# Walking the tiles of a DMA-filled kernel from the last rows to the first

## The chip, the cores and the metric

The kernel runs on one core of one Trainium2 chip. The time is that of one execution on the device, in microseconds; medians of several executions are quoted with their number. The record marks each run fast or slow by its clock and its distance from the fastest run. Data go by DMA: 16 engines move packets between the chip's main memory (HBM), which holds x and the output, and the on-chip memory (SBUF). A packet is one contiguous piece; here each transfer has one for each of the 128 partitions of SBUF.

## The reference

```python
B, S, D = 8, 512, 2048                    # x: (8, 512, 2048) float32, gamma: (2048,)
x_rep = np.repeat(x, 2, axis=1)           # each row twice: (8, 1024, 2048)
rms = np.sqrt((x_rep ** 2).mean(axis=-1, keepdims=True) + 1e-6)
return (x_rep / rms * gamma[None, None, :]).astype(np.float32)
```

It is an RMS norm of 4096 rows of 8 KB whose result is written twice, so 33.55 MB come in and 67.11 MB go out.

## The kernel before

Eight tiles of 512 rows go through three row buffers. A partition holds four neighbouring rows, so a tile is one contiguous block of 4 MB in x and of 8 MB in the output. All large transfers are issued by SyncE (`nc.sync`), in program order.

```python
K = 4                                             # P = 128 partitions, R = 2
# ...
x_t = x.rearrange("b s d -> (b s) d").rearrange("(n p k) d -> n p k d", p=P, k=K)
out_t = out.rearrange("b s d -> (b s) d").rearrange("(n p j) d -> n p (j d)", p=P, j=K * R)
# ...
rows = ctx.enter_context(tc.tile_pool(name="rows", bufs=3))
# ...
def load(i, eng, parts=1):
    y = rows.tile([P, K * R, D], f32, name="y")
    step = K // parts
    for k in range(0, K, step):
        at = K * (R - 1) + k
        eng.dma_start(out=y[:, at : at + step, :], in_=x_t[i, :, k : k + step, :])
    ys.append(y)

def store(i, k0, k1):
    nc.sync.dma_start(
        out=out_t[i, :, R * k0 * D : R * k1 * D],
        in_=ys[i][:, R * k0 : R * k1, :].rearrange("p j d -> p (j d)"),
    )
# ... (square, scale, repeat) ...
def compute(i):
    for k in range(K):
        scale(i, k, square(i, k))                 # ScalarE squares, VectorE scales
    repeat(i, 0, K // 2, nc.scalar.copy)          # second copy of each row
    repeat(i, K // 2, K, nc.vector.tensor_copy)
# ...
load(0, nc.sync, parts=2)
# ... (gamma) ...
load(1, nc.sync)
load(2, nc.sync)
# ...
loads_after = {2: (3, 4, 5), 4: (6, 7)}
for i in range(ntiles):
    compute(i)
    store(i, 0, K)
    for j in loads_after.get(i, ()):
        load(j, nc.sync)
```

The text counts loads and stores from one, in the order of issue: load 3 is `load(2)`. On the DMA queue they stand as loads 1 to 3, stores 1 to 3, loads 4 to 6, stores 4 and 5, loads 7 and 8, stores 6 to 8. The five places where the kind changes are called seams.

## Time and profile before

| | before |
|---|---|
| time, median of 3 | 239.42 us (239.32 to 239.43) |
| span of the profiled execution | 237.9 us |
| VectorE busy, ScalarE busy | 96.5 us, 101.0 us |
| share of the DMA queue of x and the output | 98.5% |
| data moved over the span | 423 GB/s |
| packets of 16, 32, 64 KB, median | 611, 1213, 2418 ns |

The table says that the 16 DMA engines are full and that no compute engine is busy for half the time. The prediction shows the lines for this. The last row comes from the packet records of the trace, which give size, start and duration of each packet. One more view: the issues of SyncE in the timeline of before (start, time from the first issue's start to the last one's end, engine and line, what, how many).

```profile
0.72 8.20 SPq L52 DMA_DIRECT2D y<-in_x_dram  x4
...
27.05 24.67 SPq L56 DMA_DIRECT2D out_dram<-y  x3
...
52.84 39.05 SPq L52 DMA_DIRECT2D y<-in_x_dram  x3
...
115.86 12.72 SPq L56 DMA_DIRECT2D out_dram<-y  x2
...
140.24 19.73 SPq L52 DMA_DIRECT2D y<-in_x_dram  x2
...
160.08 36.66 SPq L56 DMA_DIRECT2D out_dram<-y  x3
```

These six groups are the six stretches between the five seams. An issue is not the start of the transfer: the second group of loads is issued from 52.84 us on, but its first packet starts at 90.4 us, behind the stores.

### The profile page before, as it was taken

To read this page: it belongs to the slowest core of one execution; us is meant where nothing else is said; L and a number is where in the kernel's file an instruction comes from. 1 tells how busy PE (TensorE), PEld (TensorE's weight loads), DVE (VectorE), ACT (ScalarE), POOL (GpSimd) and SP (SyncE) were. 2 spreads that over 40 slices of the span, in tenths; PEclk is the share of its full clock that TensorE was granted. 3 is DMA by queue.
4 is the path that set the end of the run, shared out by engine and by line. 5 is a ranking of instruction groups with operands and counts; after the bars stand their busy time and mean duration, and the time that the engine had idled before them with its cause. 6 is when DMAs were issued, how large, how long until landed. Compare 5 with 4: busy or idle time off the path is not lost.

```text
span 237.9 us, 287 instructions
## 1 busy us (share of the span) xinstructions
DVE 96.5 (41%) x73; ACT 101.0 (42%) x106; POOL 2.5 (1%) x5
## 2 busy tenths in 40 slices
DVE  0049999960000000059999960000199990000000
ACT  2697999900000000099999920000599960000000
POOL 0030000000000000000000000000000000000000
DMA  7999998989899998999998999989998989999994
GB/s 265 436 446 441 441 441 353 530 353 496 386 452 430 397 485 353 441 441 441 441 518 364 464 419 430 452 369 430 435 518 364 518 364 485 397 452 430 408 474 176
DMA packets 2464, 100.69 MB, mean 423 GB/s; under 512 B 279, under 2 KB 285, under 8 KB 286
## 3 DMA queue, kind: packets, MB, share of 16 engines
q1 hardware_dynamic: 2448, 100.66, 98.5%
q14 instruction: 2, 0.02, 0.0%
q10 hardware_dynamic: 14, 0.01, 0.0%
HBM read 33.56 MB, written 67.11 MB: 423 GB/s over the span
## 4 chain that ended last, share of the span: by engine, by line
DMA 58%; ACT 12%; DVE 9%; issue 1%; POOLq 1%; ACTq 1%; SPq 0%
DMA y<-in_x_dram 33%; DMA out_dram<-y 21%; ACT sq L64 8%; DVE y L74 7%; DMA gamma_b<-in_gamma_dram 4%; ACT y L81 3%; DVE y L81 2%; ACT rms L68 1%; POOLq L136 1%; ACTq L95 1%; DVE rstd L73 0%; POOLq L96 0%; SPq L56 0%
## 5 line engine op out<-in xcount | busy, mean ns | idle before, releaser
L64 ACT ACTIVATE sq<-y 128x2048 f32<-128x2048 f32 x32 | 59.7, 1865 | 87.8 <-DMA y<-in_x_dram 87.8
L74 DVE SCALAR_TENSOR_TENSOR y<-y,rstd,gamma_b 128x2048 f32<-128x2048 f32 x32 | 75.3, 2352 | 4.1 <-POOL gamma_b L96 3.0
L73 DVE RECIPROCAL rstd<-rms 128x1 f32<-128x1 f32 x32 | 5.0, 158 | 94.6 <-ACT rms L68 94.3
L81 ACT COPY y<-y 128x4096 f32<-128x4096 f32 x8 | 28.7, 3590 | 1.4 <-DVE y L74 1.4
L81 DVE COPY y<-y 128x4096 f32<-128x4096 f32 x8 | 18.3, 2294 | 0.3
L68 ACT ACTIVATE rms<-ss,eps_t 128x1 f32<-128x1 f32 x32 | 9.4, 295 | 1.0
L64 ACT ACTIVATION_READ_ACCUMULATOR sq<-y 128x1 f32 x32 | 6.0, 187 | 0.0
L64 ACT ACT_TABLE_LOAD x1 | 1.3, 1283 | 3.0 <-issue 3.0
L96 POOL PARTITION_BROADCAST gamma_b<-gamma_b x1 | 2.3, 2294 | 12.2 <-DMA y<-in_x_dram 12.2
L68 ACT ACT_TABLE_LOAD x1 | 1.3, 1283 | 0.0
L98 DVE MEMSET eps_t<- 128x1 f32 x1 | 0.1, 59 | 0.8 <-PEq L125 0.8
L125 POOL MEMSET const-uint8-127<- 128x1 uint8 x1 | 0.1, 102 | 0.0
L125 POOL MEMSET const-bfloat16-1.0<- 128x1 bf16 x1 | 0.1, 101 | 0.0
L125 POOL MEMSET const-float32-0.0<- 128x1 f32 x1 | 0.1, 98 | 0.2 <-issue 0.2
L125 POOL MEMSET const-float32-1.0<- 128x1 f32 x1 | 0.1, 98 | 0.0
## 6 DMA issues: line engine op xcount, KB each, us to landing
y<-in_x_dram SPq DMA_DIRECT2D x7, 4096.0 KB, 14.6
y<-in_x_dram SPq DMA_DIRECT2D x2, 2048.0 KB, 7.4
out_dram<-y SPq DMA_DIRECT2D x8, 24.4
gamma_b<-in_gamma_dram ACTq DMA_DIRECT2D x6, 1.0 KB
gamma_b<-in_gamma_dram ACTq DMA_DIRECT2D x1, 2.0 KB
```

The lines of the kernel that those rows point to most:

```text
L64: nc.scalar.activation(out=sq[:], in_=ys[i][:, K * (R - 1) + k, :], func=Act.Square, accum_out=ss[:])
L68: nc.scalar.activation(out=rms[:], in_=ss[:], func=Act.Sqrt, scale=inv_d, bias=eps_t[:])
L73: nc.vector.reciprocal(out=rstd[:], in_=rms[:])
L74: nc.vector.scalar_tensor_tensor(out=ys[i][:, R * k, :], in0=ys[i][:, K * (R - 1) + k, :], scalar=rstd[:], in1=gamma_b[:], op0=Alu.mult, o ...
L81: copy(out=y_r[:, k0:k1, 1, :], in_=y_r[:, k0:k1, 0, :])
L95: nc.scalar.dma_start(out=gamma_b[0:1, c0:c1], in_=gamma[c0:c1].partition_broadcast(1))
L96: nc.gpsimd.partition_broadcast(out_ap=gamma_b[:], in_ap=gamma_b[0:1, :])
L98: nc.vector.memset(eps_t, eps)
L125: nc = _bacc.Bacc("TRN2", target_bir_lowering=False, num_devices=1)
L136: with _tile.TileContext(nc) as tc:
```

## The change

Its intent is to visit the same tiles in the opposite order, so that x is read and the output is written from the last rows to the first. Nothing else is touched.

```diff
-            eng.dma_start(out=y[:, at : at + step, :], in_=x_t[i, :, k : k + step, :])
+            eng.dma_start(out=y[:, at : at + step, :], in_=x_t[ntiles - 1 - i, :, k : k + step, :])
...
-            out=out_t[i, :, R * k0 * D : R * k1 * D],
+            out=out_t[ntiles - 1 - i, :, R * k0 * D : R * k1 * D],
```

## The prediction

> **What bounds the kernel now.** The kernel before takes 239.42 us (median of three, 239.32 to 239.43); its profiled execution took 239.72 us with a span of 237.9 us. I read first the shares of the engines and the timeline in 40 slices, to see whether an engine or the DMA is full.
>
> ```profile
> DVE 96.5 (41%) x73; ACT 101.0 (42%) x106; POOL 2.5 (1%) x5
> ...
> DVE  0049999960000000059999960000199990000000
> ACT  2697999900000000099999920000599960000000
> ...
> DMA  7999998989899998999998999989998989999994
> ```
>
> No compute engine is busy for half of the span, and both have long stretches of zeros. The DMA row is at 8 or 9 in every slice but the first and the last. Next, the part on DMA queues and the issues, for what that transfer time consists of:
>
> ```profile
> q1 hardware_dynamic: 2448, 100.66, 98.5%
> ...
> HBM read 33.56 MB, written 67.11 MB: 423 GB/s over the span
> ...
> y<-in_x_dram SPq DMA_DIRECT2D x7, 4096.0 KB, 14.6
> y<-in_x_dram SPq DMA_DIRECT2D x2, 2048.0 KB, 7.4
> out_dram<-y SPq DMA_DIRECT2D x8, 24.4
> ```
>
> One queue carries all of x and all of the output, and its packets fill 98.5% of the time of 16 DMA engines. The bytes are the least possible: x once (4096 x 2048 x 4 B = 33.55 MB), the output once (67.11 MB).
>
> The third reading is of the packet records in the trace, sorted by size, because a share of busy time does not say whether a packet runs at its best pace. There are three sizes that matter: 16 KB (256 packets, the two halves of the first load), 32 KB (896, the other seven loads, one packet per partition) and 64 KB (1024, the eight stores). Their medians are 611, 1213 and 2418 ns, and the median is nearly also the least: 608, 1213 and 2418 ns. So a 64 KB packet moves at 27.1 GB/s per engine and a 32 KB one at 27.0, reads and writes alike; 16 x 27.1 = 434 GB/s. If every packet ran at its median the 16 engines would need (256 x 611 + 896 x 1213 + 1024 x 2418) / 16 = 232.5 us. The packets' real durations sum to 234.2 us per engine, so all the extra time that slow packets cost is 1.7 us. First packet to last takes 235.1 us (1.7 to 236.8 us of the span), so gaps are another 0.9 us. What remains of the span is 1.7 us at the head and 1.1 us at the tail.
>
> Fourth, the waits, to see whether a transfer is ever issued too late for its place in the queue. The DMA queue's own waits:
>
> ```profile
> SPq L56 <- DVE y L81: 108.8, 7, 23.9
> SPq L52 <- DMA out_dram<-y: 69.6, 5, 19.1
> SPq L136 <- DMA out_dram<-y: 40.1, 3, 19.3
> ```
>
> These look large, but they are waits of the issuing engine, not of the transfers. I compared each issue in the timeline with when the queue before it ran dry. The first store is issued at 27.0 us, while the loads keep the engines busy to 33.0: 6 us in hand. The fourth load is issued at 52.8 us, when the first store has landed; the second and third stores run to 91.0, so 38 us in hand. The fourth store is issued at 115.9 us against loads that run to 120.1: 4 us in hand, the tightest place. The seventh load is issued at 140.2 us against 159.1, the seventh store at about 184.0 us against the end of the sixth store at 198.1. So the DMA engines never starve between the first load and the last store, and the span is a sum of transfers.
>
> The chain that ended last starts with the small loads of gamma and then goes through DMA and compute; its DMA share of 58% understates the case, since it counts a compute step as holding the chain where transfers ran beside it.
>
> **What the Trainium skill says.** "DMA: Bandwidth & Descriptors", section Bandwidth (Where 436 GB/s comes from), puts the ceiling on the SBUF side of the transfer path, 435.2 GB/s for all 16 engines. The trace agrees: 434 GB/s from the median packet, and the same pace for reads and for writes. "HBM Reference", section Specifications, says that a core streaming alone measures about 425 GB/s, bounded by its 16 DMA engines; the page of the kernel before has 423 GB/s over the span. The one statement on addresses is again in "DMA: Bandwidth & Descriptors", section Latency and other measured facts: row pitches of large powers of two (512 KiB and more) slow a copy down, and laying tiles out contiguously avoids that. Here the pitch between partitions is 32 KB in x and 64 KB in the output, each tile is one contiguous block of 4 or 8 MB, and the trace shows packets at full pace.
>
> **The change part by part.** Only the index of the tile in the two addresses changes, from i to 7 - i, in x and in the output alike. It removes and adds no instruction: the order of instructions on each engine, compared between the two built kernels, differs in line numbers alone (75 rows on VectorE, 78 on ScalarE, 9 on SyncE in both). SBUF addresses, the three row buffers, the order of issue (4 transfers in, 3 out, 3 in, 2 out, 2 in, 3 out) and every semaphore wait are the same. The sum, step by step:
>
> - Compute: 32 squares of 1865 ns, 32 scalings of 2352 ns, eight copies of 3590 ns and eight of 2294 ns are the same on the same shapes; change 0.
> - Packets at their median pace: 232.5 us before; the same number, size, contiguity and SBUF side after; change 0.
> - Relation of reads to writes: loads and stores alternate in blocks of two to four and overlap only at the five seams, by about 1 us each. A tile's base moves by a whole number of 4 MB (x) or 8 MB (output), so within a tile the lower address bits are as they were. What can differ is which parts of memory meet at a seam.
> - Slow packets: 1.7 us in all, and I can place most of them. The first half-load has a mean of 689 ns over a median of 611, so 128 x 78 / 16 = 0.6 us; the third load, just ahead of the first stores, has 1331 over 1213, so 128 x 118 / 16 = 0.9 us. The rest is about 0.1 us for any transfer. The first of these is the start-up, beside the loads of gamma, which reversed order does not touch; the second is the seam from reading to writing. Only this 0.9 us has some claim to depend on addresses. It could vanish or double.
> - Head and tail: 1.7 and 1.1 us, set by issue and by the landing of the last packet; change 0.
>
> So the sum is 0, with about 0.9 us open to either side. My estimate is 239.4 us.
>
> **The rivals.** First, addresses in memory matter: the new pairs of read and write blocks at seams, or the start of the loads at the far end of x, are slower or faster for the memory. For it speaks the third load's slow packets (up to 2335 ns for 1213). Against it, they are 0.9 us in all, four later seams show hardly any (means of 1218 and 1221 ns), and memory never sets the pace elsewhere. If every one of five seams cost 0.9 us it would be 239.4 + 4 x 0.9 = 243.0, which is still within 2%; if all slow packets went, 239.4 - 1.7 = 237.7. Second, a wait is exposed: if packets of one load were later by more than 4 us, the fourth store would leave the queue dry. Nothing moves in time here, so this needs the first rival at several times its size; 4 us of gap beyond that would make 247. Third, a benefit of reuse, in that a later execution finds the end of x or of the output in a nearer place. The profile shows no such place: loads after the first run at 1213 ns from the first tile to the last, and a packet cannot be quicker than the engine's own pace. It would make 239.4 as well. A gain of 2% would need 4.8 us, more than slow packets and gaps together (1.7 + 0.9 = 2.6 us), so the trace itself nearly excludes it.
>
> **How the range and the chances follow.** Three runs before spread over 0.11 us, and the profiled execution lay 0.3 us above their median. To that I add the open part of the seams, which I take as half of the 0.9 us to either side: 238.9 to 240.0. Slower by over 2% (244.2) takes an effect of addresses five times the one seen, on all seams or on whole tiles: 0.02. Faster by over 2% (234.6) lies only about 2 us over the 232.5 us of transfers at full pace: 0.005, and I write 0.01. The rest, 0.97, is the same.
>
> **What would show it right or wrong.** Right: 16, 32 and 64 KB packets with medians of 611, 1213 and 2418 ns again, q1 at about 98.5%, 423 GB/s, the same groups with the same means, first issues of the fourth load and fourth store near 52.8 and 115.9 us. The first rival shows as one tile, or the last packets ahead of a seam, with a mean well above the median, in tiles that before had none. The second shows as a slice of the DMA row below 8 in mid-span. The prediction is wrong if whole tiles have another median, which would mean that the place in memory sets the pace of a transfer and not the engine.

## The result, and the profile after

| | before | after |
|---|---|---|
| time, median of 6 | 239.43 us (239.32 to 239.63) | 239.43 us (239.28 to 239.87) |
| ratio after / before | | 1.0003 (95% interval 0.999 to 1.0016) |
| packets of 16, 32, 64 KB, median | 611, 1213, 2418 ns | 611, 1213, 2418 ns |
| slow packets in all, per engine | 1.76 us | 1.91 us |

Ratios and their intervals are from fast runs alone; they are not quite ratios of the medians. "Slow packets" is the sum over all packets of duration less the median of its size, divided by 16 engines.

The page of the kernel after, where it answers to the lines shown of before (engines, DMA row of the timeline, queue, data rate, issues):

```profile
DVE 96.5 (41%) x73; ACT 101.0 (43%) x106; POOL 2.5 (1%) x5
...
DMA  7999998989989898999999898989998999989894
...
q1 hardware_dynamic: 2448, 100.66, 98.7%
...
HBM read 33.56 MB, written 67.11 MB: 424 GB/s over the span
...
y<-in_x_dram SPq DMA_DIRECT2D x7, 4096.0 KB, 14.6
...
out_dram<-y SPq DMA_DIRECT2D x8, 24.3
```

All of it is nearly as it was: 98.7% against 98.5%, 424 against 423 GB/s, landing after 24.3 against 24.4 us. The engines' issues have not moved either, as the timeline of after shows:

```profile
26.86 24.66 SPq L57 DMA_DIRECT2D out_dram<-y  x3
...
52.87 39.17 SPq L53 DMA_DIRECT2D y<-in_x_dram  x3
...
115.84 12.73 SPq L57 DMA_DIRECT2D out_dram<-y  x2
```

The store that has least time in hand, the fourth, is issued at 115.84 us against 115.86.

### The profile page after: what moved, and what is told of

Read it like the earlier page. It is cut to its first block, busy times and chain, and to the rows that moved or that the text cites. A ratio compares the mean times of both kernels' runs of the same rounds, so it can differ in the third digit from the quotient of the medians.

```text
span 237.7 us, 287 instructions
## 1 busy us (share of the span) xinstructions
DVE 96.5 (41%) x73; ACT 101.0 (43%) x106; POOL 2.5 (1%) x5
## 3 DMA queue, kind: packets, MB, share of 16 engines
q1 hardware_dynamic: 2448, 100.66, 98.7%
## 4 chain that ended last, share of the span: by engine, by line
DMA 58%; ACT 12%; DVE 9%; issue 1%; POOLq 1%; ACTq 1%; SPq 0%
DMA y<-in_x_dram 33%; DMA out_dram<-y 21%; ACT sq L65 8%; DVE y L75 7%; DMA gamma_b<-in_gamma_dram 4%; ACT y L82 3%; DVE y L82 2%; ACT rms L69 1%; POOLq L137 1%; ACTq L96 1%; DVE rstd L74 0%; POOLq L97 0%; SPq L57 0%
## 6 DMA issues: line engine op xcount, KB each, us to landing
out_dram<-y SPq DMA_DIRECT2D x8, 24.3
```

## The experiments

Ten kernels were run. The question is not why the time moved but whether the reason given for its standing still is the true one: the engines' pace sets a packet's time and the place of a tile does not. The runs test the second half of this. What does set a packet's 2418 ns, the engine or something else on its way, was not tested. The main rival says that places do matter, and that this change was merely blind to it, because reads and writes were turned together or because the pattern inside a tile stayed. To compare them, the table gives the slow packets of each kernel in us per engine, worked out from the packet records of one profiled execution each, within 6 us of each seam, which is put at the first packet of the new kind.

| kernel | start | load 3 to store 1 | store 3 to load 4 | load 6 to store 4 | store 5 to load 7 | load 8 to store 6 | five seams |
|---|---|---|---|---|---|---|---|
| before | 0.63 | 0.94 | 0.00 | 0.04 | 0.03 | 0.06 | 1.07 |
| after | 0.56 | 1.18 | 0.00 | 0.01 | 0.01 | 0.08 | 1.28 |
| e1_loads_only | 0.46 | 1.11 | 0.00 | 0.01 | 0.00 | 0.07 | 1.19 |
| e9_zigzag | 0.72 | 0.86 | 0.00 | 0.03 | 0.01 | 0.07 | 0.98 |
| e3_same_tile | 0.64 | 0.96 | 0.00 | 0.01 | 0.00 | 0.15 | 1.13 |
| e2_pitch | 0.54 | 1.35 | 1.30 | 0.39 | 1.16 | 0.36 | 4.55 |
| e6_pitch_x | 0.43 | 1.43 | 0.12 | 0.03 | 0.16 | 0.37 | 2.10 |
| e7_pitch_out | 0.57 | 1.02 | 1.17 | 0.58 | 1.21 | 0.83 | 4.80 |
| e5_early_write | 0.55 | 0.94 | 0.00 | 0.01 | 0.01 | 0.02 | 0.97 |
| e4_slack_one | 0.64 | 0.96 | 0.00 | 0.01 | 0.27 | 0.90 | 2.14 |
| e4_slack_five | 0.60 | 0.84 | 0.00 | 0.05 | 0.95 | 0.87 | 2.71 |
| e8_late_first | 0.62 | 0.05 | 0.83 | 0.88 | 0.00 | 0.04 | 1.81 |

In all of them the medians of 32 and 64 KB packets over the kernel stayed at 1213 and 2418 ns.

### Half of the change alone: e1_loads_only

```diff
 # from the kernel after
-            out=out_t[ntiles - 1 - i, :, R * k0 * D : R * k1 * D],
+            out=out_t[i, :, R * k0 * D : R * k1 * D],
```

> Loads go from the last tile of x to the first, stores from the first tile of the output to the last, so the tiles come out in the wrong places (wrong result on purpose). Theory (a DMA engine sets the pace of a packet, the place in memory does not): 239.4 us, ratio 0.998 to 1.002, medians of the packets 611, 1213 and 2418 ns. Rival (places matter, and reversing reads and writes together only kept their relation): this breaks the relation, so packets at the five seams slow down, 0.9 us or more for each, 241 to 244 us.

Measured: 239.40 us (median of 5) against 239.64 us of before (9), ratio 0.9991 (0.9978 to 1.0005). Its output is wrong, which doesn't matter for the time. The seams cost 1.19 us, as in both kernels. So the two halves of the change do not hide each other's effect.

### Another order: e9_zigzag

```diff
+    order = (0, 7, 1, 6, 2, 5, 3, 4)
-            ... in_=x_t[i, :, k : k + step, :])
+            ... in_=x_t[order[i], :, k : k + step, :])
-            out=out_t[i, :, ...],
+            out=out_t[order[i], :, ...],
```

> Tiles in the order 0, 7, 1, 6, 2, 5, 3, 4, in x and output alike (result right). Theory (where a tile lies, by whole 4 or 8 MB, does not set the pace): 239.3 to 240.0 us, ratio 0.998 to 1.003. Rival (order matters, and the straight orders up and down are equal by symmetry only): over 0.5% slower, with slow packets inside tiles rather than at the seams.

Measured: correct, 239.41 us (5) against 239.50 us (9), ratio 0.9994 (0.9981 to 1.0006). An order with long jumps is as good as a straight one, so this is no matter of symmetry between up and down.

### The same 4 MB eight times: e3_same_tile

```diff
-            ... in_=x_t[i, :, k : k + step, :])
+            ... in_=x_t[0, :, k : k + step, :])
```

> Every load reads the first tile of x (wrong result on purpose), so 4 MB are read eight times. Theory: 239.4 us, ratio 0.998 to 1.002, 32 KB packets at a median of 1213 ns from first to last. Rival (what was touched lately is nearer or what lies in one place collides): another median for loads after the first; each 1% of 1213 ns would be 896 x 12 / 16 = 0.7 us of the time.

Measured: 239.47 us (5) against 239.64 us (9), ratio 0.9994 (0.9982 to 1.0007); wrong result. Reading what was read just before is neither quicker nor slower, which leaves nothing of the third rival of the prediction as far as reads go; for writes to the output it was not tested.

### Another pattern inside the tile: e2_pitch, and its halves e6_pitch_x and e7_pitch_out

```diff
-    ... .rearrange("(n p k) d -> n p k d", p=P, k=K)              # e2, e6: x
+    ... .rearrange("(p n k) d -> n p k d", p=P, k=K)
-    ... .rearrange("(n p j) d -> n p (j d)", p=P, j=K * R)        # e2, e7: output
+    ... .rearrange("(p n j) d -> n p (j d)", p=P, j=K * R)
```

Partition p now owns 32 neighbouring rows. Packets keep their sizes, but one tile's pieces lie 256 KB apart in x and 512 KB apart in the output.

> Partition p takes rows 32p to 32p+31, so a tile is 128 pieces of 32 KB, 256 KB apart, in x and of 64 KB, 512 KB apart, in the output; packets keep their sizes and the result is right. Theory: the engines' pace holds, 239.4 us, ratio 0.995 to 1.005, medians 1213 and 2418 ns. Rival (addresses do set the pace when the pattern inside a tile changes, which the reversal left alone): 64 KB packets with a median above 2490 ns and a time over 244 us.

> Only x is read with 256 KB between partitions, the output is written as before (wrong result on purpose). The kernel with both pitches was 1.8% slower, with medians unchanged and slow packets at the seams alone. If the reads are the cause: 243 to 244.5 us, about 3 us of slow packets at the later seams. If the writes: 239.4 us and at most 0.3 us there. If it takes both: under 1 us.

> Only the output is written with 512 KB between partitions, x is read as before (wrong result on purpose). If the writes are the cause of the 1.8%: 243 to 244.5 us. If the reads: 239.4 us. If it takes both: under 1 us.

Measured: both, 244.21 us (4) against 239.64 (9), ratio 1.0184 (1.0164 to 1.0203); x alone, 240.62 us (6) against 239.57 (11), ratio 1.0042 (1.0029 to 1.0056); the output alone, 243.67 us (4) against 239.57 (11), ratio 1.0165 (1.0152 to 1.0178). The last two give wrong results, as rows come out elsewhere.

Here the theory in its plain form missed: it gave e2_pitch a ratio of at most 1.005. The rival got the time right (over 244 us) and the way to it wrong, since it asked for a slower median. Of the halves, the output alone came as expected for writes as the cause (243 to 244.5 us); x alone was then expected at 239.4 us and cost 1.0 us more, so the reads have a smaller part. Both together (4.55 us at the seams) cost no more than the output alone (4.80). The DMA part of the page of e7_pitch_out tells how this looks:

```profile
DMA  7999999999999999999998989899999898989894
...
DMA packets 2464, 100.69 MB, mean 417 GB/s; under 512 B 279, under 2 KB 285, under 8 KB 286
...
q1 hardware_dynamic: 2448, 100.66, 98.6%
```

The queue's share is 98.6%, as good as before, and the DMA row has no hole; only the rate has gone from 423 to 417 GB/s. A slow packet counts as busy, so the share cannot show it. The table above does: slow packets at all five seams, 4.80 us in place of 1.07, and 4.80 - 1.07 = 3.73 us covers the 3.5 us by which the spans of the two profiled executions differ (241.4 and 237.9 us); the medians differ by 4.1 us. Stores 7 and 8, which meet no loads, have a mean of 2418 ns at the same distance of 512 KB. So the pattern inside the tile matters only near the seams, and the side of the writes makes most of it; with x alone the seams cost 2.10 us. Nor is it the issuing of transfers that slows them: load 7 of this kernel is issued at 141.73 us, and the first slow packets ahead of it start at 157.2, 2.8 us before its first packet. Why writes 512 KB apart collide with reads was not traced to a part of the memory.

### Taking and overdrawing the time in hand: e4_slack_one and e4_slack_five

```diff
         repeat(i, K // 2, K, nc.vector.tensor_copy)
+        if i == 3:
+            for _ in range(1):      # 5 in e4_slack_five
+                repeat(i, K // 2, K, nc.vector.tensor_copy)
```

> One more vector copy of 2.29 us (the same values again, result right) delays the store of the fourth tile from 115.9 to about 118.2 us, still ahead of the end of the loads at 120.1. Theory (compute and waits lie beside full DMA queues, with 4 us in hand here): 239.4 to 240.0 us. Rival (the chain through compute sets the end, as the page's chain shows it): 2.3 us more, 241.7 us.

> Five more such copies, 11.5 us, put the store of the fourth tile at about 127.3 us; [...]the queue is dry from about 119.4 to 128.5. Theory: 8.5 to 9.5 us more, 248 to 249 us, with a hole in the DMA row there and nowhere else. Rival (chain through compute): 11.5 us more, 251 us. If the time stays, the reading of the queue was wrong.

Measured: one copy, 240.59 us (4) against 239.57 (11), ratio 1.0046 (1.0031 to 1.0061); five, 249.57 us (4), ratio 1.0416 (1.0402 to 1.0429). Both are correct.

Five copies first. The timeline of e4_slack_five has the fourth store issued 11.52 us later than before (127.38 against 115.86 us), and its page has the hole in the DMA row; the time has risen by 10.0 us, not by 11.5:

```profile
127.38 12.51 SPq L56 DMA_DIRECT2D out_dram<-y  x2
```

```profile
DMA  7999989999797989999149797999999989799995
```

The first packet of that store starts at 128.22 us, 0.84 us after its issue, where the first of the 16 engines had run dry at 119.28 us (120.01 for the last). The gap is some 8.6 us, the seams cost 1.6 us more than in before (2.71 against 1.07), and the engines end with less spread among them (0.7 against 1.4 us). This is a little more than was expected, 249.57 against 248 to 249 us, and the seams explain it.

With one copy the fourth store is issued at 118.15 us:

```profile
118.15 12.51 SPq L56 DMA_DIRECT2D out_dram<-y  x2
```

Its first packet starts at 119.38 us, just as the first engine runs dry, so there is no gap, as the theory said. Yet the time is 1.0 us longer, where 239.4 to 240.0 was expected. It is not the rival's 2.3 us either. The table has it: the last two seams cost 0.27 and 0.90 us, where before they cost 0.03 and 0.06; slow packets in all are 2.84 against 1.76 us, 1.08 more. So a delay that leaves no gap can still change what later seams cost. All four runs took longer (240.44 to 241.45), so it belongs to this kernel; how it does this stays open.

### Is the first seam's cost that of the first write? e5_early_write

```diff
+    first = singles.tile([P, 128], f32, name="first")
+    nc.vector.memset(first, 0.0)
     load(0, nc.sync, parts=2)
+    nc.sync.dma_start(out=out_t[0, :, 0:128], in_=first[:])
```

> A write of 512 B per partition to the first tile of the output, issued just after the first load, and overwritten later (result right). Before and after alike lose 0.9 to 1.2 us to slow packets around 29 to 32 us, at the first seam from loads to stores, and hardly any at later ones. If that is the cost of the first writes to the output, it moves to about 12 us and mostly leaves the seam (under 0.3 us there); the time is 238.5 to 239.5 us. If it belongs to the seam itself, the seam keeps 0.9 us and the time is 239.5 to 239.9 us, longer by the small write.

Measured: correct, 239.58 us (5) against 239.64 (9), ratio 0.9999 (0.9986 to 1.0011). The first seam keeps 0.94 us, and no slow packets appear at 12 us. So it is not the cost of touching the output for the first time, at least not of a small touch.

### No meeting at the first seam: e8_late_first

```diff
         repeat(i, K // 2, K, nc.vector.tensor_copy)
+        if i == 0:
+            for _ in range(4):
+                repeat(i, K // 2, K, nc.vector.tensor_copy)
```

> Four more vector copies of 2.29 us on the first tile (the same values again, result right) put the first store at about 36.2 us instead of 27.0, so the three loads, which end near 32 to 33 us, meet no store. Before loses 0.94 us to slow packets of the third load. If reads and writes in flight together make them slow: the third load has under 0.1 us of slow packets and ends near 32.0, and the gap adds about 4 to 5 us, 243.5 to 245.5 us, and more if later seams become slow, as they did in the kernels with one and five more copies. If the slow packets belong to the moment or to the third load and not to the store: 0.9 us stays with the third load at 29 to 33 us.

Measured: correct, 246.30 us (4) against 239.50 (9), ratio 1.0283 (1.0267 to 1.0298); it was expected at 243.5 to 245.5, and at more if later seams become slow. The gap is 5.5 us per engine where 4 to 5 were expected, and slow packets are 2.62 us in all against 1.76. The page and the timeline show the hole and the late issue:

```profile
DMA  7999919798979798999999798989999999989894
```

```profile
36.34 24.66 SPq L56 DMA_DIRECT2D out_dram<-y  x3
```

Load 3 now has no slow packets and ends at 31.98 us; before, it ended at 33.01. Instead the next two seams cost 0.83 and 0.88 us, and the ones after that 0.00 and 0.04. So the cost does not belong to load 3 or to its moment: it comes where transfers of the other kind stand behind in the queue. "Reads and writes in flight together" goes a step further than the records. In before, all slow packets of load 3 start between 29.06 and 30.88 us, and the first packet of store 1 is recorded at 32.41; in e7_pitch_out, packets of load 4 are still slow at 96.0 us, when the last of store 3 ended at 92.14. But for one or two 64 KB packets, the slow ones after the start lie within 6 us of a change of kind, on both sides of it; what happens between the two kinds there is not in the trace. In before the cost is paid at the first change; after a gap it is paid again later. That the engines settle into a mutual timing in which they collide no more, and lose it in a gap, would fit this and e4_slack_five, where a gap at 119 to 128 us was followed by seams of 0.95 and 0.87. It does not explain e4_slack_one, which pays late without a gap. No run here shows it directly, and the trace does not tell which packet ran on which engine.

## Why the prediction was right

**The transfers at full pace.** The step said 232.5 us of packets at their median pace, before and after. The medians came out the same to the nanosecond, in after and in every experiment, whichever tiles were read or written. e1_loads_only, e9_zigzag and e3_same_tile show that neither the direction, nor the order, nor the pairing of reads with writes, nor the reuse of what was read has a part in it. Two small readings need mending. The slow packets are 234.21 - 232.46 = 1.76 us before rounding, not 1.7. And the 0.9 us of "gaps" is hardly any gap: from 5 to 235 us all 16 engines have a packet in the records but for 0.10 us per engine; the rest is mostly the uneven end, where the engines finish between 235.4 and 236.8 us.

**No instruction moves.** The page after has the same groups, and the issues stand within 0.2 us of where they were. Compute was predicted at a change of 0 and is 96.5 and 101.0 us again.

**The time in hand.** The step read 4 us for the fourth store, and the conclusion that no wait is exposed was right: the kernel does not respond to the direction. But the figure was too generous. It took the time at which the last engine ran dry, 120.1 us, and left out the way from issue to first packet. With 119.4 us for the first engine and the 0.84 us of e4_slack_five, the store has 119.4 - 0.84 - 115.86 = 2.7 us in hand. e4_slack_one used 2.29 of these and left no gap. The prediction's price for overdrawing them was of the right kind: five copies made a gap of 8.6 us and a time 10.0 us longer.

**The slow packets.** The prediction left 0.9 us at the first seam open, to vanish or to double; it was 1.18 in place of 0.94. It set the first 0.6 us down to the start, where it stayed (0.56). It also said that the 0.9 us alone had some claim to depend on addresses. For the order of tiles any such effect is small: the seam costs 0.86 to 1.18 us in five kernels with five different orders and pairings. The two that begin with the last tiles of x have the highest, 1.18 and 1.11, against 0.84 to 0.96 in the kernels above with before's pitch that begin with tile 0 and have a store at this seam; with one profile of each, 0.2 us more is neither shown nor excluded, and the times do not show it. For the pattern inside a tile it does depend on addresses: 1.35 and 1.43 us with x at 256 KB. And it needs a store behind the loads, as e8_late_first shows.

**The rivals.** The first rival, every seam at 0.9 us, was priced at 243.0 us. It did not come with this change, but it exists: e7_pitch_out has 4.80 us at its seams and took 243.67 us. The change moves tiles by whole blocks and leaves the pattern inside a tile alone, which that kernel does not. The argument against this rival in the prediction, that memory never sets the pace, was therefore too broad: it holds in stretches of one kind, and at the later seams only for this layout. The second rival, an exposed wait, did not come: no issue moved by more than 0.2 us. The third rival, reuse, was tested for reads by e3_same_tile and has no effect of 0.2% or more.

**Size.** The range, 238.9 to 240.0 us, rested on an effect of half a microsecond to either side; the six runs after lie from 239.28 to 239.87.

## What to carry to other kernels

In this DMA-filled kernel, whose packets nearly all run at one duration, the order in which whole contiguous blocks are visited was free, and could be chosen for other reasons. Look at the packets over the median of their size and at where they lie, not at the busy share alone, since a slow packet counts as busy, and not at the median alone, which stayed at 2418 ns in the kernel that was 1.65% slower. What was not free is the layout inside a block: writing in pieces 512 KB apart cost that 1.65% with the same packet sizes, all but a little of it at the seams between loads and stores. The time in hand before a queue runs dry is to be counted to the first engine that empties, less the time from issue to first packet.

## What the Trainium skill lacked or had wrong

- "DMA: Bandwidth & Descriptors", section Latency and other measured facts, tells of large power-of-two row pitches as a loss of rate for copies between two HBM tensors. It does not say what happens to loads and stores between HBM and SBUF. Here a stretch of stores alone at a pitch of 512 KB ran at the full 2418 ns a packet, and nearly the whole loss of 1.65% lay at the seams between loads and stores (3.73 us).
- No page tells that packets can be slow where loads and stores follow each other in the queue, with contiguous tiles too: 0.94 us per engine at the first seam of the kernel before, near 0 at the later ones, and again 0.8 to 0.95 us at two seams after a gap in the DMA queue (0.90 at one seam of e4_slack_one, without a gap).
- "DMA: Bandwidth & Descriptors", section Bandwidth (Where 436 GB/s comes from), gives a ceiling of 435.2 GB/s, and 16 engines at 64 KB in 2418 ns make 434 GB/s, reads and writes alike. But its note that the HBM side (~358 GB/s) binds transfers between HBM and SBUF does not hold for this kernel, which runs on one core: 423 and 424 GB/s over the spans. "HBM Reference", section Specifications, with its 425 GB/s for a core streaming alone, agrees.
